# A two-layer hybrid backbone: attention probabilities normalised behind the values' matmuls, and a band mask of the scores' type

## The chip, the cores and the metric

The kernel runs on one core of one Trainium2 chip. The metric is the device time of one execution in microseconds (us). Engines: TensorE (PE, with its weight loads as PEld), VectorE (DVE), ScalarE (ACT), GpSimd (POOL) and SyncE (SP, which issues most DMAs). Each engine works through its own instructions in the order in which the program issues them.

## The reference, cut to what matters

Two consecutive layers on 256 noisy latent tokens with a context of 256 tokens, model width 1024. Each layer is half a SwiGLU, token mixing, and another half SwiGLU, each with RMS norm and a modulation. The even layer mixes with a state-space scan (S5) on half of the width and dense grouped attention on the other half (8 heads of 64, 2 key heads); its context tokens read context alone, its latent tokens read both. The odd layer mixes with windowed grouped attention (16 heads, 4 key heads, a window of 128) with a sink logit per head; only its latent tokens are computed.

```python
def sink_softmax(s, sink):
    sk = jnp.broadcast_to(sink.astype(jnp.float32)[:, :, None, None], s.shape[:-1] + (1,))
    p = jax.nn.softmax(jnp.concatenate([s, sk], axis=-1), axis=-1)
    return p[..., :-1]
...
        s_loc = jnp.where(mi, gqa_scores(qi, ki), -jnp.inf)
        s_ctx = gqa_scores(qi, kc)
        p = sink_softmax(jnp.concatenate([s_loc, s_ctx], axis=-1), sink)
        return gqa_values(p[..., :span], vi) + gqa_values(p[..., span:], vc)
```

The dense attention is the same without mask and sink. All is float32.

## The kernel before

Nearly every large product is made of three float32r matmuls (`mm3`, L392 to L394): each operand is kept as a high part `hi` and the rest `lo`, and hi x hi, hi x lo and lo x hi are summed. Weights come by DMA into a ring of three raw buffers; ScalarE casts the high part (L282), VectorE (in a few cases GpSimd) subtracts for the low part (L300). The order of the work is written out by hand: instructions are issued in program order, and generators on a list `bg` are advanced by one piece at each `tick()`, which is how the scan and the norms are woven between the matmuls.

Both attentions go through `attention`. A unit is 128 queries, two query heads, and two key heads (`kvl`), so it is two sub-units; each has two score tiles. The even layer has eight units (four query tiles; the first two read 256 keys, the others 512), the odd layer eight with 512 keys. A step `s_` of the loop issues, in this order:

- `scores` of sub-unit s: per head two float32r score matmuls (L935, L938) into a PSUM bank of tag `mm` (four bufs), between them in the odd layer a bfloat16 matmul that adds the band mask to one 128-column block (L937), then the row maximum on VectorE (L939);
- `transposes` of sub-unit s - 3: the probabilities by TensorE (L986), the copy `pts` on ScalarE (L987);
- `softmax` of sub-unit s: maxima scaled on VectorE (L951), two exponentials with their sums on ScalarE (L959); then for sub-unit s - 1 the reciprocal of the sums (L971) and the normalisation of its two probability tiles (L974 on ScalarE, L976 on VectorE or GpSimd);
- every second step `values` of a whole unit: 128*64 weights, 256 moving columns into `po`, a bank of tag `ms` (two bufs, shared with the scan's `psS` and `py`), L996; then for each of two heads the high part on VectorE (L1000) and the low part (L1001);
- `tick()`: a piece of the scan in the even layer. Its rotation runs on GpSimd (L1498 to L1504), the scan and its products `pr`, `t` and `H` on VectorE (L1515 to L1529), its matmuls on TensorE (L1470, L1547), copies `Ssb` and `yt` on ScalarE (L1473, L1558). At one of the last ticks (`AH`) ScalarE's casts of the output projection's first weights are issued.

The output projection (`pwo`) follows each attention at once and takes `hi` and `lo` of all units; the last unit gives the third and fourth of the four attention blocks in the even layer, and the last two of eight in the odd layer. The masks are built once, on GpSimd, by `win_masks` (L821 to L832), early in the program, within the scan's preparation.

Of the kernel before, what the change touches and what calls it, by code (L numbers as in the profile page):

```python
# [11 lines left out]
F32 = mybir.dt.float32  # L12
F32R = mybir.dt.float32r
BF16 = mybir.dt.bfloat16
AF = mybir.ActivationFunctionType
OP = mybir.AluOpType
# [10 lines left out]
CTX, LAT = 0, 1  # L27
# [9 lines left out]
def hybrid_kernel(ctx: ExitStack, tc: tile.TileContext, x, c, ctx_in, c_ctx, mod_w, mod_b, norm_g, ffn_wg, ffn_wu,  # L37
# [58 lines left out]
    const = pool("const")  # L96
# [11 lines left out]
    def tt(name, shape, tag=None, bufs=2, dtype=F32):  # L108
        return tmp.tile(list(shape), dtype, name=name, tag=tag or name, bufs=bufs)
# [58 lines left out]
    class Operand:  # L168
# [11 lines left out]

        def __getitem__(self, ix):
            return self.t[ix[2] // 4][ix[:2] + (ix[2] % 4,) + ix[3:]]

    hh, hl = Operand("hh"), Operand("hl")

# [3 lines left out]
    def tokens(t):  # L189

        return t // 2, slice((t % 2) * 128, (t % 2 + 1) * 128)
# [624 lines left out]
                G.tensor_mul(ropeS[:, z, :, hs], rp[:, :, 32:64], gains[:, l, z, None, ho].to_broadcast([128, 2, 32]))  # L816
            G.tensor_scalar(ropeS[:, z, :, 0:32], ropeS[:, z, :, 0:32], -1.0, None, op0=OP.mult)

    masks = const.tile([128, 3, 128], BF16, name="masks")
    sinkb = const.tile([128, 2, 16], F32, name="sinkb")  # L820

    def win_masks():

        mf = tt("mf", [128, 2, 128], tag="half", bufs=3)
        G.memset(mf, 0.0)
        G.affine_select(mf[:, 0], mf[:, 0], pattern=[[-1, 128]], base=0, channel_multiplier=1,
                        compare_op=OP.is_ge, fill=NEG)
        G.affine_select(mf[:, 1], mf[:, 1], pattern=[[1, 128]], base=0, channel_multiplier=-1,
                        compare_op=OP.is_ge, fill=NEG)
        G.tensor_copy(masks[:, 0:2], mf)  # L830
        G.tensor_copy(masks[:, 2], ident)
        G.tensor_scalar(sinkb[:, 1], sinkb[:, 0], -1.0, None, op0=OP.mult)  # L832

    scr = const.tile([128, 1], F32, name="scr")

# [80 lines left out]
    def attention(ap, units, qT, rq, kTh, kTl, v, dst, pt_slots, mask=None, sinkb=None):  # L916


        subs = [(u, kvl) for u in range(len(units)) for kvl in range(2)]
        state = {}  # L920
        pt_n = [0]

        def scores(u, kvl):
            qcol, kvp, hg0, nkb, msk = units[u]
            nk = nkb * 128
            kv = kvp * 2 + kvl
            l = 0 if sinkb is None else 1
            assert ("q", l, (kv * 4 + hg0) // 8 * 8, qcol.start) in ready
            assert all(("k", l, b * 128) in ready for b in range(nkb))
            scs = []  # L930
            mx = tt("mx", [128, 8], bufs=3)
            for i in range(2):
                h = kv * 4 + hg0 + i
                sc = ps("sc")
                T.matmul(sc[:, 0:nk], qT[:, h, qcol], kTh[:, kv, 0:nk], start=True, stop=False)  # L935
                if msk is not None:
                    T.matmul(sc[:, msk[1] * 128:(msk[1] + 1) * 128], mask[:, 2], mask[:, msk[0]], start=False, stop=False)  # L937
                T.matmul(sc[:, 0:nk], qT[:, h, qcol], kTl[:, kv, 0:nk], start=False, stop=True)  # L938
                V.tensor_reduce(mx[:, i:i + 1], sc[:, 0:nk], axis=AX.X, op=OP.max)  # L939
                scs.append(sc)  # L940
            state[u, kvl] = [scs, mx, None]

        def softmax(u, kvl, prev):

            if (u, kvl) in state:
                qcol, kvp, hg0, nkb, msk = units[u]
                nk = nkb * 128
                scs, mx, _ = state[u, kvl]
                hs = slice((kvp * 2 + kvl) * 4 + hg0, (kvp * 2 + kvl) * 4 + hg0 + 2)
                rqu = rq[:, qcol.start // 128]  # L950
                V.tensor_mul(mx[:, 2:4], mx[:, 0:2], rqu[:, 1, hs])  # L951
                if sinkb is not None:
                    V.tensor_tensor(mx[:, 2:4], mx[:, 2:4], sinkb[:, 1, hs], op=OP.min)
                    G.tensor_add(mx[:, 4:6], mx[:, 2:4], sinkb[:, 0, hs])
                sm = tt("smx", [128, 8], bufs=3)
                P = []
                for i in range(2):
                    p = xt_("P", [128, 512])
                    S.activation(p[:, 0:nk], scs[i][:, 0:nk], AF.Exp, bias=mx[:, 2 + i:3 + i],  # L959
                                 scale=rqu[:, 0, hs.start + i:hs.start + i + 1],  # L960
                                 accum_out=sm[:, i:i + 1])
                    P.append(p)
                if sinkb is not None:
                    S.activation(sm[:, 2:4], mx[:, 4:6], AF.Exp)
                state[u, kvl] = [P, sm]
            if prev in state:
                P, sm = state[prev]
                nk = units[prev[0]][3] * 128
                if sinkb is not None:
                    V.tensor_add(sm[:, 0:2], sm[:, 0:2], sm[:, 2:4])  # L970
                V.reciprocal(sm[:, 4:6], sm[:, 0:2])  # L971
                for i in range(2):
                    if sinkb is None and i == 0:
                        S.activation(P[i][:, 0:nk], P[i][:, 0:nk], AF.Copy, scale=sm[:, 4:5])  # L974
                        continue
                    (G if i else V).tensor_scalar(P[i][:, 0:nk], P[i][:, 0:nk], sm[:, 4 + i:5 + i], None, op0=OP.mult)  # L976

        def transposes(u, kvl):
            P, sm = state[u, kvl]
            nkb = units[u][3]  # L980
            pts = pt_slots[pt_n[0] % len(pt_slots)]
            pt_n[0] += 1
            for i in range(2):
                pt = ps("ppt", "tp")
                for kb in range(nkb):
                    T.transpose(pt[:, kb * 128:(kb + 1) * 128], P[i][:, kb * 128:(kb + 1) * 128], ident)  # L986
                S.copy(pts[:, 0:nkb, i * 128:(i + 1) * 128], pt[:, 0:nkb * 128].rearrange("p (b q) -> p b q", b=nkb))  # L987
            state[u, kvl] = pts

        def values(u):  # L990
            qcol, kvp, hg0, nkb, msk = units[u]
            po = ps("po", "ms")
            for kb in range(nkb):
                for kvl in range(2):
                    kv = kvp * 2 + kvl
                    T.matmul(po[kvl * 64:kvl * 64 + 64, 0:256], v[:, kb, kv * 64:kv * 64 + 64], state[u, kvl][:, kb, :],  # L996
                             start=kb == 0, stop=kb == nkb - 1, tile_position=(0, kvl * 64))
            for i in range(2):
                hi, lo = dst(u, i)
                V.tensor_copy(hi, po[:, i * 128:(i + 1) * 128])  # L1000
                V.tensor_sub(lo, po[:, i * 128:(i + 1) * 128], hi.bitcast(F32))  # L1001

        n = len(subs)
        l = 0 if sinkb is None else 1
        TL, dp, sf = TLS[l], DP[l], SF[l]
        for s_ in range(n + TL):
            if s_ < n and sf:
                scores(*subs[s_])
            if s_ >= TL:
                transposes(*subs[s_ - TL])  # L1010
            if s_ < n and not sf:
                scores(*subs[s_])
            c_ = s_ - dp
            if 0 <= c_ <= n:
                softmax(*(subs[c_] if c_ < n else (-1, 0)), subs[c_ - 1] if c_ else None)
            if s_ >= TL + 2 and (s_ - TL) % 2 == 0:
                values(subs[s_ - TL - 2][0])
            tick()
        values(subs[n - 1][0])


# [12 lines left out]
    def s5_prep(pp):  # L1034
# [44 lines left out]
        for _ in range(6):  # L1079
            yield  # L1080
        rope_tables(0)
        win_masks()
        ee = pt_("ee", [128, 1])
        G.memset(ee, math.e)
        dP = pt_("dP", [32, 2])
# [338 lines left out]
    def mixer_ab(nm, ap, nxt):  # L1424
# [220 lines left out]
        for t in range(4):  # L1645
            s_, tl = tokens(t)
            pq = ps("pq")
            for i in range(2):
# [6 lines left out]
                if i:  # L1655
# [3 lines left out]

        units = [(slice(qt * 128, (qt + 1) * 128), 0, hg0, 4 if qt >= 2 else 2, None) for qt in range(4) for hg0 in (0, 2)]  # L1660
        attention(ap, units, qT, rq, kTh, kTl, v,
                  lambda u, i: tuple(z[:, u // 4, 4 + units[u][2] + i, tokens(u // 2)[1]] for z in (hh, hl)),
                  [z[:, s_] for z in (hh.renew(0, F32), hl.renew(0, F32)) for s_ in (CTX, LAT)])
        gc = ap.tile([128, 2, 2, 4, 256], F32R, name="gc", tag="big")

# [93 lines left out]
    def mixer_win(nm, ap, nxt):  # L1759
# [2 lines left out]
        v = ap.tile([128, 4, 256], F32, name="v1")  # L1762
        qT = ap.tile([128, 16, 256], F32R, name="qT1")
        rq = ap.tile([128, 2, 2, 16], F32, name="rq1")
        ckv = [use(("wkv", 0), pre=MW == 0 or WA == 0)]
        pk = [ps("pkv1") for _ in range(4)]
        for s_ in (CTX, LAT):
# [34 lines left out]
                        tick()  # L1802
        if WX:
            warm(AF.Exp)
        units = [(slice(qt * 128, (qt + 1) * 128), kvp, hg0, 4, (0, 3) if qt == 0 else (1, 2))
                 for kvp in range(2) for qt in range(2) for hg0 in (0, 2)]
        attention(ap, units, qT, rq, kTh, kTl, v,
                  lambda u, i: tuple(z[:, LAT, units[u][1] * 4 + units[u][2] + i, units[u][0]] for z in (hh, hl)),
                  [ap.tile([128, 4, 256], F32, name="pts%d" % i) for i in range(4)], mask=masks, sinkb=sinkb)
        fsl = [slice(0, 128), slice(128, 256)]  # L1810
        for dp in range(4):
# [169 lines left out]
```

## Time and profile before

| what | us |
|---|---|
| median of 3 runs (lowest to highest) | 1765.82 (1763.88 to 1766.41) |
| the profiled execution, its time | 1764.65 |
| its span, first to last instruction | 1762.9 |
| TensorE busy in the span | 1710.4 (97%) |
| VectorE busy | 1080.0 (61%) |
| ScalarE busy | 633.9 (36%) |
| GpSimd busy | 425.1 (24%) |

Times in the rows are from the start of the span. The even layer's attention lies from about 519 to 607 us, the odd layer's from about 1480 to 1539. A recorded duration runs to the end of the instruction's last write, so that the next instruction of an engine often starts before it; a step from start to start is what an engine pays. The matmuls' ends are modelled.

### The profile page before, as it was taken

What the parts mean: (1) busy time and instruction counts of PE and PEld (TensorE: products, weight loads), DVE (VectorE), ACT (ScalarE), POOL (GpSimd) and SP (SyncE); (2) the same over time, 40 slices, a digit from 0 to 9 for tenths busy, and PEclk for the clock granted to TensorE, in tenths of its full rate; (3) what the DMA queues carried; (4) which work ended last, traced back from release to release, by engine and by line L of the source; (5) the groups of instructions that cost most, each with busy time, mean ns of one, the idle gap of its engine ahead of it and who ended that gap; (6) DMA issues with size and microseconds to landing.
All of it is one profiled execution on the core that took longest, in us unless ns stands there. A gap on an engine that the chain in (4) does not pass through costs nothing.

```text
span 1762.9 us, 25224 instructions
## 1 busy us (share of the span) xinstructions
PE 1710.4 (97%) x9951; PEld 1430.8 (81%) x9951; DVE 1080.0 (61%) x1802; ACT 633.9 (36%) x1210; POOL 425.1 (24%) x565
## 2 busy tenths in 40 slices
PE   6999999999988899999999999999999998999998
PEld 4778888878976689888888898888888886699998
DVE  5566768566578755576556554754546378755455
ACT  3322222223445643222222243222222257754443
POOL 5314768522367303000000022000000046620000
PEclk8999999999997999999999999999999999999999
DMA  8546575596544524464445323454645224045653
GB/s 261 183 139 173 160 211 178 177 296 215 162 144 131 138 75 166 150 201 136 158 137 162 108 95 114 156 184 145 213 149 163 95 96 96 1 144 169 205 176 120
DMA packets 209454, 272.60 MB, mean 155 GB/s; under 512 B 23673, under 2 KB 171385, under 8 KB 208825
## 3 DMA queue, kind: packets, MB, share of 16 engines
q1 hardware_dynamic: 204912, 261.26, 46.9%
q10 hardware_dynamic: 3064, 5.32, 0.8%
q0 software_dynamic: 1360, 4.42, 0.7%
q8 instruction: 78, 1.28, 0.3%
q14 instruction: 40, 0.32, 0.1%
HBM read 255.77 MB, written 15.17 MB: 154 GB/s over the span
## 4 chain that ended last, share of the span: by engine, by line
PE 84%; DVE 7%; DMA 3%; issue 2%; ACT 2%; POOL 1%; SPq 0%; ACTq 0%; POOLq 0%; DVEq 0%
PE pu L392 16%; PE pu L393 15%; PE pu L394 15%; PE pd L392 7%; PE pd L394 7%; PE pd L393 7%; PE pwo L392 1%; PE pwo L394 1%; PE pwo L393 1%; PE pm L453 1%; PE pacc L392 1%; PE pacc L393 1%; PE pacc L394 1%; DVE H L1529 1%; PE po L996 1%
## 5 line engine op out<-in xcount | busy, mean ns | idle before, releaser
L392 PE MATMUL pu<-hh,whi 128*128 128x512 f32 (+1 forms) x1392 | 505.6, 363 | 3.2 <-ACT hh L549 2.9
L393 PE MATMUL pu<-hl,whi 128*128 128x512 f32 (+1 forms) x1392 | 500.9, 360 | 2.7 <-DVE hl L551 2.6
L394 PE MATMUL pu<-hh,wlo 128*128 128x512 f32 (+1 forms) x1392 | 500.3, 359 | 0.0
L300 DVE TENSOR_TENSOR wlo<-raw,whi 128x1024 fp32r<-128x1024 f32 (+2 forms) x314 | 356.4, 1175 | 42.5 <-ACT whi L282 41.9
L282 ACT CAST whi<-raw 128x1024 fp32r<-128x1024 f32 (+1 forms) x310 | 293.9, 997 | 245.6 <-PE pd L393 158.0
L392 PEld LDWEIGHTS pu<-hh,whi 128*128 128x128 f32 x1392 | 263.7, 189 | 51.2 <-issue 5.3
L393 PEld LDWEIGHTS pu<-hl,whi 128*128 128x128 f32 x1392 | 263.9, 190 | 41.0 <-DVE hl L551 3.5
L394 PEld LDWEIGHTS pu<-hh,wlo 128*128 128x128 f32 x1392 | 263.6, 189 | 39.6 <-DVE wlo L300 0.2
L506 POOL TENSOR_TENSOR acc<-acc,sq 128x256 f32<-128x256 f32 x54 | 41.9, 779 | 784.7 <-ACT sq L512 784.2
L392 PE MATMUL pd<-ahi,whi 128*128 128x512 f32 (+1 forms) x624 | 224.8, 360 | 0.0
L598 DVE TENSOR_TENSOR hm<-sg,pu 128x512 f32<-128x512 f32 (+1 forms) x88 | 54.4, 618 | 275.7 <-PE pu L394 275.6
L394 PE MATMUL pd<-ahi,wlo 128*128 128x512 f32 (+1 forms) x624 | 222.7, 357 | 0.0
L393 PE MATMUL pd<-alo,whi 128*128 128x512 f32 (+1 forms) x624 | 222.6, 357 | 0.0
L227 ACT CAST ahi<-hm 128x512 fp32r<-128x512 f32 (+1 forms) x88 | 49.9, 567 | 367.0 <-DVE hm L598 367.0
L485 DVE SCALAR_TENSOR_TENSOR ma<-mraw,silc,ma 128x1024 f32<-128x1024 f32 (+1 forms) x126 | 142.3, 1160 | 5.7 <-DMA mraw<-in_mod_w_dram 5.4
L392 PEld LDWEIGHTS pd<-ahi,whi 128*128 128x128 f32 x624 | 117.9, 189 | 20.6 <-issue 3.3
L589 DVE SCALAR_TENSOR_TENSOR xT<-pd,m,xT 128x256 f32<-128x256 f32 x192 | 84.6, 478 | 78.6 <-PE pd L394 78.3
L394 PEld LDWEIGHTS pd<-ahi,wlo 128*128 128x128 f32 x624 | 117.9, 189 | 17.6 <-DVE wlo L300 0.5
L393 PEld LDWEIGHTS pd<-alo,whi 128*128 128x128 f32 x624 | 117.9, 189 | 16.5
L594 ACT ACTIVATE sg<-pu 128x512 f32<-128x512 f32 (+1 forms) x88 | 47.6, 544 | 230.0 <-PE pu L394 229.5
L228 DVE TENSOR_TENSOR alo<-hm,ahi 128x512 fp32r<-128x512 f32 (+1 forms) x88 | 56.4, 641 | 55.7 <-ACT ahi L227 55.7
L549 ACT ACTIVATE hh<-h,m 128x256 fp32r<-128x256 f32 x88 | 41.6, 503 | 59.8 <-DVE h L542 59.8
(375 smaller groups left out, 2452.4 us busy)
## 6 DMA issues: line engine op xcount, KB each, us to landing
raw<-in_ffn_wg_dram SPq DMA_DIRECT2D x44, 1024.0 KB, 5.4
raw<-in_ffn_wu_dram SPq DMA_DIRECT2D x44, 1024.0 KB, 5.4
mraw<-in_mod_w_dram SPq DMA_DIRECT2D x72, 512.0 KB, 5.2
raw<-in_mod_w_dram SPq DMA_DIRECT2D x32, 1024.0 KB, 5.1
raw<-in_ffn_wd_dram SPq DMA_DIRECT2D x36, 768.0 KB, 4.5
raw<-in_ffn_wd_dram SPq DMA_DIRECT2D x17, 1024.0 KB, 5.0
raw<-me_d SPq DMA_DIRECT2D x8, 768.0 KB, 5.2
raw<-in_win_w_in_dram SPq DMA_DIRECT2D x6, 1024.0 KB, 5.2
```

The source lines that it names most:

```text
L227: (S.copy if eng is None else eng.tensor_copy)(dst_hi, src)
L228: V.tensor_sub(dst_lo, src, dst_hi.bitcast(F32))
L282: S.copy(ph, src)
L300: eng.tensor_sub(pl_, src, ph.bitcast(F32))
L392: T.matmul(o, lhs[0], rhs[0], start=start, stop=False)
L393: T.matmul(o, lhs[0], rhs[1], start=False, stop=False)
L394: T.matmul(o, lhs[1], rhs[0], start=False, stop=stop)
L485: V.scalar_tensor_tensor(ma[c0, s_], raw[i], silc[:, k, s_:s_ + 1], ma[c0, s_], op0=OP.mult, op1=OP.add)
L506: G.tensor_add(acc[s_], acc[s_], sq_late.pop(s_))
L589: V.scalar_tensor_tensor(xT[:, d, sl], psrc, m[:, l, j, d, s_:s_ + 1], xT[:, d, sl], op0=OP.mult, op1=OP.add)
L594: S.activation(sg, pg, AF.Silu)
L598: V.tensor_mul(hm, sg, pu)
```

## The change

The probabilities stay unnormalised through transposes and values' matmuls. Each unit keeps its inverse sums in a tile `inv` (one per unit, [128, key head, head]). Behind the values' matmuls four small matmuls spread them: the weights are one column of inverse sums repeated 64 times, the moving operand the identity, so that the upper half of `po`'s bank holds, for each of the 64 rows of a head and each query, its inverse sum. The upper half is copied to SBUF (`rb`), multiplied with the lower half into `o`, from which `hi` is copied and `lo` subtracted, each for both heads of the unit in one instruction. In the even layer `rb` and `hi` are copied by ScalarE, in the odd layer by VectorE; the multiplication is VectorE's, the subtraction GpSimd's.

The mask becomes float32r, as the scores are: four blocks (band, zero, band, identity), of which two adjoining ones are added to columns 256 to 511 in one matmul of 256 columns. It is built at the odd layer's start in that layer's pool, on GpSimd; the negated sink alone is still made early.

```diff
+        def pair(self, s_, k, tok):
+            return self.t[k // 4][:, s_, k % 4:k % 4 + 2, tok]
...
+    def win_masks(ap):
+        mf = ap.tile([128, 2, 128], F32, name="mf", tag="pts3")
         G.memset(mf, 0.0)
...
-        G.tensor_copy(masks[:, 0:2], mf)
-        G.tensor_copy(masks[:, 2], ident)
-        G.tensor_scalar(sinkb[:, 1], sinkb[:, 0], -1.0, None, op0=OP.mult)
+        masks = ap.tile([128, 4, 128], F32R, name="masks")
+        for i in range(2):
+            G.tensor_copy(masks[:, 2 - 2 * i], mf[:, i])
+        G.tensor_scalar(masks[:, 1], ident, 0.0, None, op0=OP.mult)
+        G.tensor_copy(masks[:, 3], ident)
+        return masks
...
-                    T.matmul(sc[:, msk[1] * 128:(msk[1] + 1) * 128], mask[:, 2], mask[:, msk[0]], start=False, stop=False)
+                    T.matmul(sc[:, 256:512], mask[:, 3], mask[:, msk:msk + 2], start=False, stop=False)
...
-                V.reciprocal(sm[:, 4:6], sm[:, 0:2])
-                for i in range(2):
-                    if sinkb is None and i == 0:
-                        S.activation(P[i][:, 0:nk], P[i][:, 0:nk], AF.Copy, scale=sm[:, 4:5])
-                        continue
-                    (G if i else V).tensor_scalar(P[i][:, 0:nk], P[i][:, 0:nk], sm[:, 4 + i:5 + i], None, op0=OP.mult)
+                if prev[1] == 0:
+                    inv[prev[0]] = tt("inv", [128, 2, 2], bufs=4)
+                V.reciprocal(inv[prev[0]][:, prev[1]], sm[:, 0:2])
...
+            r = inv.pop(u)
             for i in range(2):
-                hi, lo = dst(u, i)
-                V.tensor_copy(hi, po[:, i * 128:(i + 1) * 128])
-                V.tensor_sub(lo, po[:, i * 128:(i + 1) * 128], hi.bitcast(F32))
+                for kvl in range(2):
+                    T.matmul(po[kvl * 64:kvl * 64 + 64, 256 + i * 128:384 + i * 128], r[:, kvl, i:i + 1].to_broadcast([128, 64]),
+                             ident, start=True, stop=True, tile_position=(0, kvl * 64))
+            rb = tt("rb", [128, 256], tag="acc%d" % (u % 2), bufs=1)
+            (S.copy if sinkb is None else V.tensor_copy)(rb, po[:, 256:512])
+            o = tt("ao", [128, 256], tag="h", bufs=2)
+            V.tensor_mul(o, po[:, 0:256], rb)
+            o = o.rearrange("p (i q) -> p i q", i=2)
+            hi, lo = dst(u)
+            (S.copy if sinkb is None else V.tensor_copy)(hi, o)
+            G.tensor_sub(lo, o, hi.bitcast(F32))
...
         rope_tables(0)
-        win_masks()
+        G.tensor_scalar(sinkb[:, 1], sinkb[:, 0], -1.0, None, op0=OP.mult)
...
         rq = ap.tile([128, 2, 2, 16], F32, name="rq1")
+        masks = win_masks(ap)
         ckv = [use(("wkv", 0), pre=MW == 0 or WA == 0)]
```

## Rows read from the trace of the kernel before

**Rows 1.** Windows: busy time (and count) of each engine, granted clock, DMA.
```profile
570.00:592.00 22.00, 19.37 (x145) 13.45 (x143) 21.42 (x56) 13.59 (x30) 12.66 (x12) 0.92 0.46 120
592.00:608.00 16.00, 13.02 (x110) 9.74 (x109) 8.29 (x23) 13.99 (x28) 4.70 (x3) 0.89 0.46 108
...
1498.00:1530.00 32.00, 32.00 (x232) 21.77 (x230) 28.82 (x96) 28.18 (x76) 20.32 (x22) 1.00 0.01 2
```
**Rows 2.** Chain that ended last, even layer: start, us, what.
```profile
590.10 1.21 DVE mx L939 x2
...
593.24 0.61 ACT P L974
...
602.11 1.31 PE py L1547 x24
...
607.54 0.23 PE pwo L393
```
**Rows 3.** Timeline, one step of the even layer: start, us, engine, line.
```profile
575.22 0.16 DVE L951 TENSOR_TENSOR mx<-mx,rq 128x2 f32<-128x2 f32 x1
...
575.38 0.27 DVE L1000 CAST hh<-po 128x128 fp32r<-128x128 f32 x1
...
576.42 1.26 DVE L1515 TENSOR_TENSOR_SCAN uu<-rhoT,uu 128x256 f32<-128x256 f32 x2
576.91 0.23 ACT L959 ACTIVATION_READ_ACCUMULATOR P<-sc,mx,rq 128x1 f32 x1
...
577.60 0.89 DVE L1524 TENSOR_TENSOR pr<-uu,tbl 128x256 f32<-128x256 f32 x1
```
**Rows 4.** Groups by line, VectorE, 526 to 592: busy, mean ns, idle before.
```profile
L1525 DVE TENSOR_TENSOR t<-uu,tbl 128x256 f32<-128x256 f32 x12 | 7.3, 610 | 0.0
L1524 DVE TENSOR_TENSOR pr<-uu,tbl 128x256 f32<-128x256 f32 x12 | 6.9, 573 | 0.0
...
L1000 DVE CAST hh<-po 128x128 fp32r<-128x128 f32 x10 | 2.8, 278 | 2.7 <-PE po L996 2.7
```
**Rows 5.** Groups by line, ScalarE, 515 to 608.
```profile
L1558 ACT COPY yt<-py 128x256 f32<-128x256 f32 x8 | 2.6, 380 | 0.0
```
**Rows 6.** Timeline, a VectorE operation with one operand in PSUM.
```profile
1424.52 0.47 DVE L542 SCALAR_TENSOR_TENSOR h<-xT,m,pn 128x256 f32<-128x256 f32 x1
```
**Rows 7.** Timeline, GpSimd's normalisation beside a VectorE product.
```profile
572.05 1.83 POOL L976 TENSOR_SCALAR P<-P,smx 128x512 f32<-128x512 f32 x1 [2.49 <-PE po L996]
572.11 0.42 DVE L1525 TENSOR_TENSOR t<-uu,tbl 128x256 f32<-128x256 f32 x1
```
**Rows 8.** Line 554, a GpSimd subtraction: ns min/median/max.
```profile
L554 POOL TENSOR_TENSOR hl<-h,hh x18: 728/742/1605, 445.0 to 1571.8; 128x256 fp32r<-128x256 f32 x18
```
**Rows 9.** Timeline, the even layer's tail.
```profile
600.80 2.00 ACT L282 CAST whi<-raw 128x1024 fp32r<-128x1024 f32 x2
...
604.05 1.07 ACT L987 COPY hl<-ppt 128x512 f32<-128x512 f32 x2 [1.25 <-PE ppt L986]
...
607.04 0.50 PE L392 MATMUL pwo<-hh,whi 128*128 128x512 f32 x1
```
**Rows 10.** Timeline, one masked score and the transposes behind it.
```profile
1502.34 0.40 PE L935 MATMUL sc<-kTh,qT 128*128 128x512 f32 x1
...
1502.94 1.03 PE L986 MATMUL ppt<-ident,P 128*128 128x128 f32 x8
```
**Rows 11.** Chain, the odd layer's output projection (256 columns).
```profile
1538.99 0.32 PE pwo L392
...
1541.22 0.12 PE pwo L394
```
**Rows 12.** Timeline of GpSimd, three places; brackets: idle time before, releaser.
```profile
41.79 0.76 POOL L1087 TENSOR_TENSOR dP<-ee,lsP 32x2 f32<-32x2 f32 x1 [7.51 <-DMA lsP<-in_s_log_step_dram]
...
1433.58 0.70 POOL L553 TENSOR_TENSOR h<-h,m 128x256 f32<-128x256 f32 x1 [2.46 <-ACT hh L549]
...
1538.02 4.75 POOL L300 TENSOR_TENSOR wlo<-raw,whi 128x1024 fp32r<-128x1024 f32 x2 [3.97 <-ACT whi L282]
```

More of the change, by code (lines that the diff above doesn't have):

```diff
@@ L817, in rope_tables @@
             G.tensor_scalar(ropeS[:, z, :, 0:32], ropeS[:, z, :, 0:32], -1.0, None, op0=OP.mult)
-    masks = const.tile([128, 3, 128], BF16, name="masks")
     sinkb = const.tile([128, 2, 16], F32, name="sinkb")
-    def win_masks():
-        mf = tt("mf", [128, 2, 128], tag="half", bufs=3)
+    def win_masks(ap):
+        mf = ap.tile([128, 2, 128], F32, name="mf", tag="pts3")
         G.memset(mf, 0.0)
@@ L919, in attention @@
         subs = [(u, kvl) for u in range(len(units)) for kvl in range(2)]
-        state = {}
+        state, inv = {}, {}
         pt_n = [0]
@@ L967, in softmax @@
                 P, sm = state[prev]
-                nk = units[prev[0]][3] * 128
                 if sinkb is not None:
                     V.tensor_add(sm[:, 0:2], sm[:, 0:2], sm[:, 2:4])
-                V.reciprocal(sm[:, 4:6], sm[:, 0:2])
-                for i in range(2):
-                    if sinkb is None and i == 0:
-                        S.activation(P[i][:, 0:nk], P[i][:, 0:nk], AF.Copy, scale=sm[:, 4:5])
-                        continue
-                    (G if i else V).tensor_scalar(P[i][:, 0:nk], P[i][:, 0:nk], sm[:, 4 + i:5 + i], None, op0=OP.mult)
+                if prev[1] == 0:
+                    inv[prev[0]] = tt("inv", [128, 2, 2], bufs=4)
+                V.reciprocal(inv[prev[0]][:, prev[1]], sm[:, 0:2])
         def transposes(u, kvl):
@@ L1661, in mixer_ab @@
         attention(ap, units, qT, rq, kTh, kTl, v,
-                  lambda u, i: tuple(z[:, u // 4, 4 + units[u][2] + i, tokens(u // 2)[1]] for z in (hh, hl)),
+                  lambda u: tuple(z.pair(u // 4, 4 + units[u][2], tokens(u // 2)[1]) for z in (hh, hl)),
                   [z[:, s_] for z in (hh.renew(0, F32), hl.renew(0, F32)) for s_ in (CTX, LAT)])
@@ L1804, in mixer_win @@
             warm(AF.Exp)
-        units = [(slice(qt * 128, (qt + 1) * 128), kvp, hg0, 4, (0, 3) if qt == 0 else (1, 2))
+        units = [(slice(qt * 128, (qt + 1) * 128), kvp, hg0, 4, 1 - qt)
                  for kvp in range(2) for qt in range(2) for hg0 in (0, 2)]
         attention(ap, units, qT, rq, kTh, kTl, v,
-                  lambda u, i: tuple(z[:, LAT, units[u][1] * 4 + units[u][2] + i, units[u][0]] for z in (hh, hl)),
+                  lambda u: tuple(z.pair(LAT, units[u][1] * 4 + units[u][2], units[u][0]) for z in (hh, hl)),
                   [ap.tile([128, 4, 256], F32, name="pts%d" % i) for i in range(4)], mask=masks, sinkb=sinkb)
```

## The prediction

> **What bounds the kernel now.** I read the windows first, since the change touches two short stages and an average over the span says nothing of them. In the grid attention of the odd layer TensorE is the bound: from 1498 to 1530 it is busy for the whole of the stretch [rows 1], so there each matmul added costs its length and each normalisation removed on another engine gives nothing. In the dense attention of the even layer it is another engine: VectorE is busy for 21.42 of 22 us from 570 to 592, TensorE for less, and only from 592 on does VectorE fall to 8.29 of 16 [rows 1]. The chain of waits agrees: it runs on VectorE up to the row maxima at 590.10, then goes over to ScalarE (the normalisation at 593.24 is on it) and to TensorE, which it stays on from 602 to the output projection [rows 2]. VectorE is full there because the state-space scan of the other head group runs in the same steps.
>
> So three things have to be priced: VectorE's time in the even layer, the tail of that layer, and TensorE's time in the odd layer.
>
> **The even layer, VectorE's order.** Before, a pair of heads leaves VectorE four instructions: they start at 575.38, just behind the row maximum's scaling at 575.22, and the next scan starts at 576.42 [rows 3], so a unit takes 1.04 us. They read only the values' bank, which was long done. Now one multiplication stands in this place. It needs `rb`, and ScalarE copies `rb` in program order behind the two exponentials of the same step, which themselves wait for VectorE's scaling at 575.22. In the trace those exponentials' last sum is read at 576.91 and ends at 577.14 [rows 3]; I take the next free place at 577.0, since recorded ends overlap the next start. A ScalarE copy of 128x256 out of PSUM takes 0.38 [rows 5], a VectorE operation of 128x256 with one operand in PSUM 0.47 [rows 6]. The multiplication would end near 577.85, and VectorE's queue goes on 1.4 us later than before: the wait costs more than the three saved instructions. What is queued behind it is the scan, its products and the next row maxima, on which ScalarE's exponentials wait in turn.
>
> Five units have their copies before 592 (ten casts) [rows 4]. In one of them VectorE waited 2.7 us for TensorE anyway [rows 4]: I count nothing there. Two have 512 keys: 2 x 1.4. Two have 256 keys, where the exponentials are shorter: I take 1.0 each (estimate). Sum +4.8 us. From below, if the copy were always ready first, each unit would save 1.04 - 0.47 = 0.57, five units -2.9.
>
> **GpSimd's relief.** The products `pr` and `t` take 0.573 and 0.610 us in the mean [rows 4], against 0.42 for one that meets nothing of the kind [rows 7]; the one at 577.60, which meets a product on GpSimd, took 0.89 [rows 3]. Over 12 of each that is 1.8 and 2.3, together about 4.1 us that VectorE loses beside GpSimd. The change takes 16 multiplications off GpSimd here, and the rotation's products run earlier, part of them inside VectorE's new waits. But a subtraction of 0.74 us [rows 8] per unit comes to GpSimd, with two operands in SBUF as the rotation's products have. The bounds are 0 and 4.1; I take -2.5, nearer to the upper, since the waits are empty time.
>
> What the removed multiplication itself did to VectorE is seen at 572.05: it ran 1.83 us, and the VectorE product that started 0.06 us later took 0.42 [rows 7], no more than undisturbed. The Trainium skill, "SBUF — State Buffer", section "SBUF: two separate sides", says that VectorE operations with two SBUF inputs and GpSimd operations exclude one another, the later one waiting for the whole of the earlier. By that rule the product would have waited until 573.88; this row disagrees for this pair, while the row at 577.60 agrees for two products. If the rule held for all, the removal would free more of VectorE than I count (the second rival).
>
> **The even layer's tail.** ScalarE's normalisation of 0.61 on the chain at 593.24 goes [rows 2]: -0.6. Then ScalarE's order matters. Two casts of the output projection's weights ran at 600.80 for 2.00 us, while TensorE was still at the last but one unit, and the last transposes' copy came at 604.05 [rows 9]. These casts are issued in the same step behind `values`. Now `rb` and `hi` of that unit stand before them, and `rb` waits for the values and the broadcasts. The scan's output matmuls follow these values on TensorE from 602.11 [rows 2], so with 0.22 for the broadcasts they end near 602.3; `rb` 0.38, the multiplication 0.47, `hi` 0.38 and three handovers bring the casts to 603.7 to 605.7, and the last copy starts there and not at 604.05: +1.65. The last four broadcasts lie on TensorE's path: +0.25. The projection began at 607.04 on a step of 0.23 [rows 9, 2]; its seventh weight pair needs the last unit's `lo`, which now comes behind copy, multiplication, copy and 0.74 us on GpSimd, 2.3 us with handovers, where TensorE arrives after 1.4 to 1.6: +0.6. Tail: -0.6 + 1.65 + 0.25 + 0.6 = +1.9.
>
> Even layer: 4.8 - 2.5 + 1.9 = +4.2 us.
>
> **The odd layer.** Four broadcasts per unit, 128*64 weights with 128 moving columns in float32: the scan's output matmuls have that form, 24 in 1.31 us [rows 2], 0.055 each. Eight units: 32 x 0.055 = +1.8. From above, the transposes of 128x128, eight in 1.03 [rows 10], 0.13 each: +4.1. Below this there is nothing to hide it, TensorE has no idle time. A rule would put it higher: the Trainium skill, "FP8 and Floating Point Precision", section "TensorE Precision Notes", gives true float32 four passes; by that 128 columns would take 4 x 128 / 2.4 GHz = 0.21 us and a unit, with two halves side by side, 0.43, and the sum would be 1.6 higher. The 0.055 of this kernel's own rows disagrees.
>
> The mask: a score with its mask takes 0.60 us from start to start (1502.34 to 1502.94) [rows 10], two score matmuls at 0.23 [rows 2] leave 0.14 for the bfloat16 mask and what it does to its neighbours' weight loads. The new one has 256 float32r columns; that form runs at 0.12 in the projection [rows 11]. 32 masks: -0.6. From above, if it takes a full 0.23, +2.9. The removed normalisations on VectorE and GpSimd and the copies that become a multiplication lie under TensorE: 0. At the end of this stage the new chain is some 2 us long and TensorE has 18 matmuls of 0.12, 2.2 us, before it wants the last pair: 0, with no cover left. The weights' second parts on GpSimd (4.75 us for two from 1538.02) [rows 12] now queue behind `lo` and end about 3 us later, near 1546. The projection starts at 1539.0 and, 48 matmuls of 0.12 and then 15 more later [rows 11], wants their second half near 1546.5: 0, and up to 2 if it is later.
>
> Odd layer: 1.8 - 0.6 = +1.2 us.
>
> **Building the masks.** Early, GpSimd waited 7.51 us for a DMA at 41.79 behind this code [rows 12]: moving it away gives 0. In the odd layer GpSimd idled 2.46 us before 1433.58 [rows 12], and seven operations (a memset, two selects, four copies) of some 0.3 each fit there: 0, and at most 0.5 if they start late, when the norm's operations queue behind them.
>
> **Sum.** 4.2 + 1.2 = +5.4 us on the profiled execution's 1764.65, that is 1770.0. The profiled execution lies 1.2 below the median of 1765.82, inside the spread of the runs; the difference is 0.3%. A change of 0.2%, 3.5 us, is about what a measurement here tells from none.
>
> **Rivals.** One: faster. VectorE lags behind ScalarE at every unit, so that `rb` is ready when the multiplication's turn comes. Then five units give -2.9 in place of +4.8 and GpSimd's relief comes whole, 4.1: -2.9 - 4.1 + 1.9 + 1.2 = -3.9, 1760.8. For it speaks that ScalarE loses 16 normalisations here; against it that the exponentials start from VectorE's own result of the same step, so ScalarE can't be ahead. It decides once VectorE comes to the multiplication some 2 us (575.4 to 577.4) later in the step than now. Chance 0.15.
>
> Two: no difference. The wait is there, but the relief is whole, and as large again on the scan's writes of `H` (an estimate, as they meet the same products): 8.2 in place of 2.5, 5.4 - 5.7 = -0.3, 1764.4. This is what the page's lock would come to here, bounded by what VectorE's rows have in excess. With partial relief (from 4.4) it ends below 0.2% too. Chance 0.28.
>
> Three: slower still. In the odd layer the broadcasts and the mask cost their upper bounds: +2.3 and +3.5 more, 1775.8. For it speaks that TensorE has no slack there; against it, that both forms have rows of their own. Chance 0.10.
>
> My forecast, 1770.0, has 0.47. Its own range is 1768.2 to 1773. The range for all but 2 in 10 reaches into the second rival and part of the third: 1763 to 1775. Slower by over 0.2%: 0.57, within 0.28, faster 0.15.
>
> **What would show it.** VectorE should stand idle some 1 to 1.5 us before each multiplication in the even layer, with ScalarE's `rb` as releaser; the weights' casts should start behind the last but one `hi`, TensorE should wait about 0.6 at the projection's start; `pr` and `t` should be shorter in the mean. In the odd layer each unit's cycle should grow by about 0.15, with the mask's step near 0.12. I am wrong if VectorE waits for nothing there, or if the odd layer's stage changes by more than 3 us.

## The result, and the profile after

The changed kernel takes 1788.03 us (median of four runs, 1786.23 to 1788.69) against 1765.11 before (one run more than ahead of the prediction): ratio 1.0127, 95% interval [1.0115, 1.0139]. The forecast was 1770.0: slower as it said, but by 23 us and not by 5, and outside its range. The profiled execution took 1788.33 (span 1786.5, 23.6 more than before).

Where the span grew is found by laying the two traces' matmuls side by side: how much later does the same matmul start in the changed kernel? The lag, in us:

| Matmul (start before) | lag | grown in this stretch |
|---|---|---|
| keys and values of the even layer (520) | 3.1 | 3.1, in the down-projections of the first feed-forward layer, 1.4 of it in one jump at 229 |
| last scan matmuls beside the even layer's attention (598) | 7.8 | 4.7 |
| first of the even layer's output projection (607.04, [rows 9]) | 11.3 | 3.5 |
| end of that projection (649) | 12.4 | 1.1 |
| end of the two middle feed-forward layers (1425) | 17.8 | 5.4, in their down-projections |
| the odd layer's norm (1436) | 19.5 | 1.7 |
| first of the odd layer's output projection (1538.99, [rows 11]) | 22.3 | 2.8 |
| end | 23.6 | 1.3, in the last feed-forward layer |

So 9.8 of the 23.6 us (3.1 + 5.4 + 1.3) lie in layers in which the change doesn't touch an instruction. The jump at 229 is TensorE waiting for the split of the hidden activations on ScalarE and VectorE; the other 8.4 us creep up matmul by matmul. The even layer lost 9.3, the odd layer 4.5.

The windows answer to [rows 1]: busy time of TensorE, weight loads, VectorE, ScalarE, GpSimd, then the granted clock, over the same work.

```profile
576.50:601.00 24.50, 19.21 (x151) 12.78 (x151) 20.27 (x45) 12.20 (x29) 10.23 (x13) 0.94 0.41 107
601.00:619.30 18.30, 13.78 (x140) 10.22 (x139) 7.04 (x19) 12.03 (x27) 1.45 (x2) 0.99 0.52 126
1517.80:1551.80 34.00, 34.00 (x272) 26.98 (x270) 23.99 (x77) 28.51 (x76) 5.62 (x16) 1.00 0.01 1
```

VectorE, full in this stage before, now idles 4.2 of 24.5 us; TensorE is still full in the odd layer, and takes 34 us for what took 32. What VectorE waits for stands in its groups by line (529 to 603), which answer to [rows 4]:

```profile
L1540 DVE TENSOR_TENSOR H<-pr,t 64x128 f32<-64x128 f32 (+2 forms) x39 | 18.9, 511 | 0.7
...
L1535 DVE TENSOR_TENSOR pr<-uu,tbl 128x256 f32<-128x256 f32 x12 | 7.2, 596 | 0.0
L1536 DVE TENSOR_TENSOR t<-uu,tbl 128x256 f32<-128x256 f32 x12 | 7.1, 592 | 0.0
...
L1008 DVE TENSOR_TENSOR ao<-po,rb 128x256 f32<-128x256 f32 x5 | 2.1, 424 | 10.6 <-ACT rb L1006 10.6
```

10.6 us of idle time before five multiplications, all ended by ScalarE's `rb`; `pr` and `t` are not shorter. In the kernel before, the ten subtractions that stood beside the ten casts of [rows 4] were:

```profile
L1001 DVE TENSOR_TENSOR hl<-po,hh 128x128 fp32r<-128x128 f32 x10 | 2.9, 292 | 0.3
```

One unit in the timeline (it answers to [rows 3, 7]; the step has two exponentials):

```profile
569.65 0.82 ACT L965 ACTIVATE P<-sc,mx,rq 128x512 f32<-128x512 f32 x1
569.81 1.07 PE L1003 MATMUL po<-ident,inv 128*64 128x128 f32 x8
...
570.93 0.37 ACT L1006 COPY rb<-po 128x256 f32<-128x256 f32 x1 [0.36 <-PE po L1003]
...
571.40 0.42 DVE L1008 TENSOR_TENSOR ao<-po,rb 128x256 f32<-128x256 f32 x1 [3.74 <-ACT rb L1006]
...
571.86 0.40 ACT L1011 CAST hh<-ao 128x256 fp32r<-128x256 f32 x1 [0.56 <-DVE ao L1008]
...
572.34 1.18 POOL L1012 TENSOR_TENSOR hl<-ao,hh 128x256 fp32r<-128x256 f32 x1 [4.79 <-ACT hh L1011]
...
573.48 0.91 POOL L1509 TENSOR_TENSOR uu<-Ssb,tbl 128x256 f32<-128x256 f32 x1
```

Read it downwards: exponentials, `rb`, multiplication, cast, subtraction are one chain over ScalarE, VectorE, ScalarE and GpSimd. At its end GpSimd has stood 4.79 us with the subtraction at the head of its queue, and the scan's rotation (L1509), which has nothing to do with it, starts behind it. The eight broadcasts took 1.0 us here, as TensorE's granted clock was 0.50, its lower level, from 568 to 572 after it had waited 3.6.

The chain that ended last now passes over ScalarE's `rb` in seven of the eight units, where before it ran along VectorE [rows 2]:

```profile
580.50 1.30 DVE mx L945 x2
582.02 1.63 ACT P L965 x4
583.65 0.27 ACT rb L1006
583.98 0.30 issue
584.28 1.26 DVE uu L1526 x2
...
606.26 0.27 ACT rb L1006
606.55 0.44 DVE ao L1008
607.01 0.40 ACT hh L1011
607.42 0.49 ACT hh L989
607.96 1.14 PE ppt L988 x8
609.10 1.88 PE po L998 x16
610.98 0.44 PE po L1003 x8
```

From 606.26 on it is the tail: even the copy of the transposes (L989) now stands behind `rb`, multiplication and cast. The tail in the timeline (answers to [rows 9]):

```profile
612.73 0.41 ACT L1011 CAST hh<-ao 128x256 fp32r<-128x256 f32 x1 [0.56 <-DVE ao L1008]
613.04 1.99 ACT L286 CAST whi<-raw 128x1024 fp32r<-128x1024 f32 x2
...
614.93 1.06 ACT L989 COPY hl<-ppt 128x512 f32<-128x512 f32 x2
...
618.35 0.50 PE L396 MATMUL pwo<-hh,whi 128*128 128x512 f32 x1
...
620.72 0.50 PE L397 MATMUL pwo<-hl,whi 128*128 128x512 f32 x1 [0.30 <-POOL hl L1012]
```

One unit of the odd layer on TensorE (answers to [rows 10]), first before, then after. From `po` at 1523.71 to the next score at 1526.02 it is 2.31 us; the same stretch took 1.88 before (1510.10 to 1511.98). A score with its mask takes 0.58 (1526.71 to 1527.29), 0.60 before [rows 10].

```profile
1510.10 1.95 PE L996 MATMUL po<-pts,v 128*64 128x256 f32 x16
1511.98 0.50 PE L935 MATMUL sc<-kTh,qT 128*128 128x512 f32 x1
```

```profile
1523.71 1.95 PE L998 MATMUL po<-pts,v 128*64 128x256 f32 x16
1525.49 0.61 PE L1003 MATMUL po<-ident,inv 128*64 128x128 f32 x8
1526.02 0.50 PE L941 MATMUL sc<-kTh,qT 128*128 128x512 f32 x1
...
1526.71 0.40 PE L941 MATMUL sc<-kTh,qT 128*128 128x512 f32 x1
1526.94 0.28 PE L943 MATMUL sc<-masks 128*128 128x256 f32 x1
1527.06 0.39 PE L944 MATMUL sc<-kTl,qT 128*128 128x512 f32 x1
1527.29 1.03 PE L988 MATMUL ppt<-ident,P 128*128 128x128 f32 x8
```

GpSimd at the start of the odd layer (answers to [rows 12]): the mask build fits into no gap. It follows L558, and the norm's power L535, for whose result TensorE waits, follows it:

```profile
1452.20 0.84 POOL L558 TENSOR_TENSOR hl<-h,hh 128x256 fp32r<-128x256 f32 x1
1452.97 0.31 POOL L828 MEMSET mf<- 128x256 f32 x1
...
1454.85 0.28 POOL L837 CAST masks<-ident 128x128 fp32r<-128x128 f32 x1
1455.10 0.72 POOL L535 TENSOR_TENSOR rr<-rs,mhalf 128x2 f32<-128x2 f32 x1
```

Last, a line that no change was made to: 88 matmuls of the last feed-forward layer (shortest, median and longest duration in ns, then the first and the last start), of the kernel before and then of the changed one. From the first to the last of them, 163.0 us became 164.2.

```profile
L392 PE MATMUL pacc<-whi,ahi x88: 389/389/396, 1594.1 to 1757.1; 128*128 128x512 f32 x88
```

```profile
L396 PE MATMUL pacc<-whi,ahi x88: 390/393/404, 1616.7 to 1780.9; 128*128 128x512 f32 x88
```

### The profile page after: what moved, and what is told of

Its sections match the earlier page's. It is cut to its first block, busy times and chain, and to the rows that moved or that the text cites. A ratio compares the mean times of both kernels' runs of the same rounds, so it can differ in the third digit from the quotient of the medians.

```text
span 1786.5 us, 25343 instructions
## 1 busy us (share of the span) xinstructions
PE 1725.5 (97%) x10079; PEld 1441.2 (81%) x10079; DVE 1071.8 (60%) x1754; ACT 631.7 (35%) x1210; POOL 385.6 (22%) x551
## 4 chain that ended last, share of the span: by engine, by line
PE 84%; DVE 8%; ACT 3%; DMA 2%; issue 2%; POOL 1%; SPq 0%; POOLq 0%; ACTq 0%; DVEq 0%
PE pu L396 15%; PE pu L397 15%; PE pu L398 15%; PE pd L396 7%; PE pd L398 7%; PE pd L397 7%; PE pwo L397 1%; PE pwo L396 1%; PE pwo L398 1%; DVE H L1540 1%; PE pm L457 1%; PE pacc L398 1%; PE pacc L397 1%; PE pacc L396 1%; DMA me_d<-Et 1%
## 5 line engine op out<-in xcount | busy, mean ns | idle before, releaser
L553 ACT ACTIVATE hh<-h,m 128x256 fp32r<-128x256 f32 x88 | 41.6, 503 | 61.1 <-DVE h L546 61.1
```

## The experiments

### The layers that were not changed: placement in SBUF

SBUF is the memory in which the tiles lie. The masks left the constants (768 bytes of a partition) and the inverse sums came to the small tiles (128). Every tile allocated behind them moved: the weights' `whi` by 768 bytes, the feed-forward layers' hidden activations `ahi` by 640. By the sizes of the tiles in the program their distance was a multiple of 512 and is now 128 more than one.

**The change with the addresses of before:**

```diff
+    G.memset(const.tile([128, 160], F32, name="padc"), 0.0)
...
-                    inv[prev[0]] = tt("inv", [128, 2, 2], bufs=4)
+                    inv[prev[0]] = const.tile([128, 2, 2], F32, name="inv", bufs=4)
```

> The changed kernel with 640 bytes of filler in the constants and the inverse sums' four buffers beside them: every tile from the residual stream to the hidden activations then lies at the address it had before the change; the instructions are the same. Placement theory (the 9.8 us that the feed-forward layers lost come from where the operands lie in SBUF): the down-projections' 512-column matmuls return from 229 to 226 ns and the time to about 1778 us (1788.0 - 9.8). Rival (the feed-forward layers lose time to something else that the change brought, and the addresses are a coincidence): the time stays at 1788 and the 229 ns stay.

1778.81 us, ratio to before 1.0078 [1.0063, 1.0093]: 9.2 less. In the feed-forward layers the lag no longer creeps up (7.9 us at 649 and at 1425; the others show single jumps of 0.4 and less), and the line above is back at 163.1 us:

```profile
L396 PE MATMUL pacc<-whi,ahi x88: 389/389/396, 1608.5 to 1771.6; 128*128 128x512 f32 x88
```

Placement holds, the rival falls. Its odd layer lost 4.5 us where the changed kernel lost 2.8: around its first scores TensorE's clock was granted at 0.79 and 0.87 (five-us windows), where the kernel before had 1.00. The excess lies there: from 1480 to 1500 the lag grows by 2.0, in the changed kernel by 0.4.

```profile
1495.00:1500.00 5.00, 2.14 (x9) 0.79 0.06 13
1500.00:1505.00 5.00, 4.90 (x25) 0.87 0.00 0
```

**The kernel before, moved.** The same fillers, in its constants (`padc`) and behind its small tiles (`padt`), and nothing else. 256 bytes in the constants and 128 behind the small tiles:

```diff
+    G.memset(tmp.tile([128, 32], F32, name="padt"), 0.0)
+    G.memset(const.tile([128, 64], F32, name="padc"), 0.0)
```

> The kernel before, with 256 bytes of filler in the constants and 128 behind the small tiles: no instruction of the change, but modulo 1024 the operands lie as in the changed kernel. Placement theory: the down-projections slow to 229 ns and the time rises from 1765 to about 1775 (3.1 + 5.4 + 1.3 us, and perhaps 1 more in attention). Rival (not placement, or placement in units other than 1024 bytes): 1765.

1773.5, ratio 1.0045 [1.003, 1.006]. Only the 128 bytes behind the small tiles, so that the hidden activations move and the weights stay:

> The kernel before, with 128 bytes of filler behind the small tiles only: the hidden activations move by 128 bytes and the weights stay. If the down-projections' moving operand is what counts (by its own address or by its distance to the weights), about 1775 as in the run above; if the weights' address counts, 1765.

1771.82, ratio 1.0038 [1.0023, 1.0053], like the run above below the 1775 expected. 128 bytes in the constants, so that all of them move together:

> The kernel before, with 128 bytes of filler in the constants: weights, hidden activations and residual stream all move by 128 bytes and keep their distances. If the distance between the two operands counts, 1765; if the address of the moving operand itself counts, about 1775, and the gate and up projections (whose operands move too this time) may slow as well.

1764.11, ratio 0.9996 [0.9986, 1.0006]: nothing. So it is not the address of the hidden activations that counts but their distance to tiles ahead of the filler; the weights, which the slowed matmuls read with them, are among these. Then three more distances, by 64, 256 and 512 bytes behind the small tiles:

> The kernel before, with 64 bytes of filler behind the small tiles: the distance from the weights to the hidden activations becomes 64 modulo 512 (0 in the kernel before, 128 in the changed one). If any distance that is no multiple of 512 (or of 256) slows the down-projections: 1770 to 1774, 229 ns. If only some do: 1765.

> The same with 256 bytes: distance 256 modulo 512. If the unit is 256 bytes (or less), 1765 and 226 ns; if it is 512, 1770 to 1774.

> The same with 512 bytes: distance 0 modulo 512 and 512 more modulo 1024. If the unit is 512 bytes or less, 1765; if it is 1024, 1770 to 1774.

With 64 bytes 1768.78, ratio 1.0021 [1.0011, 1.003], below the 1770 to 1774 expected of a loss; with 256 bytes 1764.9, 1.0002 [0.9993, 1.0012]; with 512 bytes 1764.62, 1.0001 [0.9992, 1.001]. The line of the 88 matmuls with 64 and then with 256 bytes:

```profile
L392 PE MATMUL pacc<-whi,ahi x88: 393/398/398, 1597.0 to 1761.4; 128*128 128x512 f32 x88
```

```profile
L392 PE MATMUL pacc<-whi,ahi x88: 389/389/396, 1595.5 to 1758.6; 128*128 128x512 f32 x88
```

164.4 and 163.1: of the distances tried, multiples of 256 bytes cost nothing, 64 and 128 cost 4 and 7 us. The step from one start to the next tells the same: over 1275 steps of the 512-column down-projections of the first three feed-forward layers the median is 227 ns in the kernel before and with 256, 512 and all moved, 232 in the changed kernel and in the two runs with 128, and 229 with 64. In the last layer it goes from 227 to 232 with 128 and to 235 with 64. (The 229 ns of the expectations is the most frequent step with 128, not the middle one; many are at 237 and 238.) Why the hardware does so no run shows.

### The parts of the change, with the addresses of before

All that follow start from the run at 1778.8. **The mask build issued later**, behind the keys' and values' projections:

```diff
-        masks = win_masks(ap)
         ckv = [use(("wkv", 0), pre=MW == 0 or WA == 0)]
...
+        masks = win_masks(ap)
         for hf in range(2):
             pq = [ps("pq1") for _ in range(2)]
```

> The changed kernel with the addresses of before, and the building of the band masks issued behind the keys' and values' projections instead of ahead of them. Theory (the build's 2.1 us on GpSimd stand ahead of the norm's power L535, for which TensorE waits at the start of the odd layer): L535 starts again within some 0.5 us of its input, the 1.7 us at the start of that layer go, time 1778.8 - 1.7 = 1777.1. Rival (GpSimd is loaded there too, and the build only delays the keys' norms): 1778.8.

1777.53, ratio 1.0074 [1.0059, 1.0089]. The two intervals overlap, so the times alone settle nothing; the trace does: L535 starts 0.43 us behind L558, and the lag over this stretch goes from 9.69 to 9.66 where it had grown by 1.7.

```profile
1444.03 0.83 POOL L558 TENSOR_TENSOR hl<-h,hh 128x256 fp32r<-128x256 f32 x1
1445.30 0.71 POOL L535 TENSOR_TENSOR rr<-rs,mhalf 128x2 f32<-128x2 f32 x1 [0.43 <-DVE rs L533]
```

**One layer normalised as before, the other as changed** (the condition for the first run; the second has `is not None`; the end of `values` branches alike):

```diff
+                if sinkb is None:
+                    nk = units[prev[0]][3] * 128
+                    V.reciprocal(sm[:, 4:6], sm[:, 0:2])
...
+                else:
+                    if prev[1] == 0:
...
```

> The changed kernel with the addresses of before, and the even layer normalised as before the change (probabilities scaled on ACT and GpSimd, the two copies and subtractions on DVE out of the bank): the odd layer's part and the masks alone. If the layers' losses stand side by side, the even layer gives back its 8.1 us: 1770.7. Rival (a good part of these 8.1 us does not come from the even layer's new normalisation): above 1774.

> The changed kernel with the addresses of before, and the odd layer normalised as before the change, the new masks left in: the even layer's part and the masks alone. By eight units at 0.40 us the odd layer gives back 3 us, and up to 4.5 with the slow start of its first units in the run that is compared: 1774.3 to 1775.8. Rival (the 0.40 us of a unit come from the wider masks, not from the broadcasts): 1778.8.

The odd layer's part alone: 1770.91, ratio 1.0036 [1.0023, 1.0049], 7.9 us less than both. The even layer's part alone: 1775.92, ratio 1.0065 [1.005, 1.008], 2.9 less. The losses add. In the second run the lag grows by 1.1 at the first scores of the odd layer and then stays within 0.2 over seven units: the wider mask costs nothing there, and the 0.40 us a unit are the broadcasts'.

**Broadcasts by transposes**, four instructions in place of eight:

```diff
-                for kvl in range(2):
-                    T.matmul(po[kvl * 64:kvl * 64 + 64, 256 + i * 128:384 + i * 128], r[:, kvl, i:i + 1].to_broadcast([128, 64]),
-                             ident, start=True, stop=True, tile_position=(0, kvl * 64))
+                for kvl, pr in ((1, 128), (0, 64)):
+                    T.transpose(po[0:pr, 256 + i * 128:384 + i * 128], r[:, kvl, i:i + 1].to_broadcast([128, pr]), ident)
```

> The changed kernel with the addresses of before, and the inverse sums spread by transposes (one over 128 rows, one over the lower 64, for each half) instead of four float32 matmuls, each of which is two instructions of TensorE: four instructions for a unit instead of eight. Theory (the broadcasts cost what their instructions cost, 0.53 us a unit): 0.27 us a unit, 2.1 us less in the odd layer, and less than 1 in the even layer, which is bound by waits: 1776 to 1777. Rival (the broadcasts hide behind DVE's waits, and the unit's 0.40 us come from elsewhere): 1778.8.

1780.14, ratio 1.0093 [1.0073, 1.0112]: no gain, against the 1776 to 1777 expected. The unit in its timeline:

```profile
1522.32 1.95 PE L999 MATMUL po<-pts,v 128*64 128x256 f32 x16
1524.20 0.65 PE L1004 MATMUL po<-ident,inv 128*128 128x128 f32 x4
1524.60 0.47 PE L942 MATMUL sc<-kTh,qT 128*128 128x512 f32 x1
```

2.28 us from `po` to the next score, against 2.31: a transpose costs 0.10 where an instruction of the float32 matmul on half the columns costs 0.05. Halving the count halves nothing.

### The even layer: which wait

Base: the run with the late mask build, 1777.5. **GpSimd's subtraction one step later:**

```diff
-            G.tensor_sub(lo, o, hi.bitcast(F32))
+            held.append(lambda: G.tensor_sub(lo, o, hi.bitcast(F32)))
...
         for s_ in range(n + TL):
+            while held:
+                held.pop(0)()
```

> The changed kernel with the addresses of before and the masks built late (1777.5 us measured), and in the even layer GpSimd's subtraction of the low part issued at the start of the next step, but for the last unit. Theory A (the loss sits on GpSimd: at the head of its queue the subtraction waits for the cast on ACT, 3.7 us before 567.99, with the scan's rotation products queued behind it, and these then run late beside VectorE): the products start some 3 us earlier at that unit, and 4 to 6 us of the even layer's 8 to 9 go: 1772 to 1773.5. Theory B (the loss is VectorE's own wait for the copy rb on ACT, 12.5 us by the rows of the changed kernel): at most 1 us goes, 1776.5 to 1777.5.

**`rb` copied by VectorE, the subtraction where it was:**

```diff
-            (S.copy if sinkb is None else V.tensor_copy)(rb, po[:, 256:512])
+            V.tensor_copy(rb, po[:, 256:512])
```

> The same base, and in the even layer the broadcast sums are copied by VectorE itself, as in the odd layer, instead of by ACT; the cast of the high part stays on ACT. Theory B (VectorE's wait for ACT): VectorE waits for TensorE alone again and pays 0.42 us a unit for the copy: 3 to 5 us go, 1772.5 to 1774.5. Theory A (GpSimd's queue behind the cast, which still stands behind the exponentials on ACT): at most 1 us goes, 1776.5 to 1777.5.

**Copy, multiplication, cast and subtraction one step later** (the same list, holding all four):

> The same base, and in the even layer everything behind the broadcasts (copy, multiplication, cast, subtraction) issued at the start of the next step, but for the last unit. Both waits go: by A and B alike the even layer keeps only its broadcasts and its tail, some 1 to 3 us, and the time is 1770 to 1772. If neither wait is what costs (rival C: TensorE's lower clock and the broadcasts themselves), 1776 or more.

They gave 1774.82 (ratio 1.006 [1.0045, 1.0075]), 1770.28 (1.0031 [1.002, 1.0042]) and 1768.44 (1.0023 [1.0013, 1.0033]): 2.7, 7.2 and 9.1 us back. The first lies between its two theories, the others 2.2 and 1.6 us below the ranges expected. The first's interval overlaps the base's [1.0059, 1.0089].

The times also hold something that is not the even layer's. In all three traces the stretch of lower clock between the two middle feed-forward layers, near 1062, is shorter than in the base, and the lag falls by 1.6 there (granted clock from 1064 to 1084, by ten us: 0.81 and 0.85 in the base, 0.83 and 1.00 in the first of the three). So the traces are read for the even layer alone, as the growth of the lag from 520 to 649: 9.4 in the base (8.1 to 9.4 in the runs whose even layer is the changed kernel's), then 6.6, 1.0 and 2.2.

VectorE's waits from 526 to 606, in the base and in the second of them (total, times, longest):

```profile
DVE ao L1009 <- ACT rb L1007: 12.1, 6, 3.3
```

```profile
DVE rb L1007 <- PE po L1004: 7.0, 2, 5.2
```

Six waits for ScalarE became two for TensorE, and the kernel before has two there as well (7.7 us, one of them in [rows 4], the other in the tail). Theory B is right: the copy's place behind the exponentials is what costs, more than I expected of it. The gain lies ahead of the tail: by the last scan matmuls (598) the lag has grown by 5.4 in the base and has shrunk by 2.9 with the copy on VectorE, while the tail from there to 649 costs 4.0 and 3.9. Only the run with all four later shortens the tail, to 1.7, though VectorE still waits 8.6 us for `rb` in it, three times.

GpSimd's queue is real but second: moving the subtraction gives 1.5 to 2.8 us by the lag while B's wait stands, and VectorE's scan, `pr`, `t` and `H` take 52.5 us from 500 to 620 in place of the base's 54.6. With that wait gone the move gives nothing that shows, as the last run says.

**The best of the parts.** The even layer as in the third of these runs, the odd layer's normalisation as before, the mask late:

> The even layer as in the run above, the odd layer's normalisation as before the change, the masks new and built late, the addresses of before: the best that the parts found so far make. If the parts add, 2.9 us (the odd layer's part as measured) below the run above: 1767 to 1769, no better than the kernel before, since the even layer gains nothing by the change. Rival (GpSimd and ACT, freed of the normalisations, give time back once the waits are gone): under 1764.

1765.65, ratio 1.0004 [0.9995, 1.0014]: no difference from the kernel before, and less than the 1767 to 1769 expected, by about the 1.6 us near 1062 that its trace shows too. **The same with `rb` on VectorE and only the subtraction later:**

> The even layer with the copy of the broadcast sums on VectorE and GpSimd's subtraction issued in the next step, the odd layer's normalisation as before the change, the new masks built late, the addresses of before: both waits of the even layer removed at their cheapest. From the run with the copy on VectorE (1770.3), 2.9 us less for the odd layer and up to 2 less for the subtraction: 1765.4 to 1767.4. Rival (once the waits are gone, the relief of GpSimd and ACT that the prediction had counted at 2.5 us shows): 1761 to 1763, faster than both kernels.

1767.25, ratio 1.0017 [1.0007, 1.0026], what the parts add up to (1770.3 - 2.9). With the waits removed or shortened at two prices, neither kernel beats the one before. From 520 to 598 the lag shrinks by 1.8 and 0.6 (by 0.6 also in the kernel before with 512 bytes of filler), and the tail costs 1.8 and 3.1 again. GpSimd's relief is not in it: VectorE's scan, `pr`, `t` and `H`, 53.6 us before, take 54.9 and 55.5.

## Why the prediction was wrong

The direction was right, and so were several sizes; that the kernel became slower is no proof of the sum, since the largest part of the loss stands in none of its terms. Point by point, with the forecast of each term:

- **VectorE's wait: right.** Forecast: `rb` some 2.0 us behind the place of the old copies in units of 512 keys, 1.4 net; 1.0 net with 256. Measured in the changed kernel: 1.89 to 1.94 and 1.51 to 1.52 of idle time. The unit counted at nothing, because it waited 2.7 already, waited 3.74. All five: 10.6 - 2.7 of idle time more, and 5.7 - 2.1 of instructions less, +4.3 us against a forecast of +4.8. The run with the copy on VectorE shows that this wait is what costs.
- **GpSimd's relief: the first step that failed.** Forecast -2.5; `pr` and `t` together went from 14.2 to 14.3 us, and `H` grew from 466 to 511 ns in the mean of the same 39. The sentence that the products would "run earlier, part of them inside VectorE's new waits" had it the wrong way round: the subtraction waits at the head of GpSimd's queue for the end of the same chain, the rotation runs later, and when VectorE goes on it meets it. What was queued behind the added instruction was asked for VectorE and ScalarE in the even layer, not for GpSimd. The products of the runs with the waits removed or shortened are no shorter either; only the subtraction moved by itself brings scan, `pr`, `t` and `H` below the kernel before, by 1.1 us.
- **The even layer's tail: +4.6 for +1.9.** The casts' 1.65 was right (1.57). The normalisation that left ScalarE did not give -0.6: `rb`, the multiplication and the cast took its place ahead of the transposes' copy, +1.0. The broadcasts of two units lie on the path at 0.5 and 0.44, not one at 0.25. The stalls in the projection came to 1.1 for 0.6. (The chain before does not stay on TensorE from 602, as the prediction reads it: ScalarE's copy at 604.05 [rows 9] is on it.)
- **The odd layer: +2.8 for +1.2.** The broadcasts were mis-sized: 0.43 us a unit (2.31 - 1.88) for 0.22. The row used was right, 0.055 for an instruction of that form; the count was not. A float32 matmul of the program is two instructions in the trace (x8 for a unit's four), as the values' x16 for eight matmuls show. The Trainium skill, "FP8 and Floating Point Precision", "TensorE Precision Notes", gives true float32 four passes, from which the prediction estimated 0.43 a unit; it set the trace against that, and the trace, rightly counted, agrees with it. The mask is a little cheaper than the old one (0.58 for 0.60 a score), as forecast, and its range's upper end was not touched.
- **The mask build: +1.7 for 0.** The gap of 2.46 us that was to take it lies ahead of L553 (L557 in the changed kernel); the code issues the build behind the subtraction L558 that follows, next to the power on which the norm hangs. The idle time was real, but not at this place in the queue. The late build shows it.
- **Untouched layers: +9.8, in no term and no rival.** The largest part: the prediction put them at nothing without a reason. It priced instructions alone; that tiles allocated anew move all others was not asked. Of the 9.8, 8.4 creep up in the down-projections as placement makes them, and the runs with moved tiles give 7 to 9 for it. The jump of 1.4 at 229 is not shown to be placement.

The rivals: VectorE never came to the multiplication after `rb`, so the first fell; the relief of the second, 8.2, came in no run; the third was half right, in that the broadcasts went towards their upper bound (3.5 for 4.1). Of the two signs of being wrong neither came by its letter: VectorE did wait, and the odd layer's stage grew by 2.8, under 3 (4.5 with the mask build). By the lags, the even layer up to its tail, the tail, the odd layer, the mask build and the untouched layers make 4.7 + 4.6 + 2.8 + 1.7 + 9.8 = 23.6 us, the growth of the span.

## What to carry to other kernels

A change that adds, drops or moves a tile shifts every tile allocated behind it: compare the same untouched matmuls in both traces before explaining a difference by the change, and try a filler that restores the addresses. For an instruction added to a chain over several engines, write down for each of them what stands behind it in program order: here a copy cheap in itself cost 7 us by its place behind two exponentials, and a mask build cost 1.7 by its place ahead of a power. And count a matmul's instructions in the trace, not in the program.

## What the runs showed of the hardware

The 512-column float32r matmuls of the down-projections run slower when the hidden activations lie 64 or 128 bytes further from the weights in SBUF than in the kernel before, where the distance is a multiple of 512: with 128 their median step from one start to the next went from 227 to 232 ns, that is 7 to 9 us of this kernel; at 0, 256 and 512 bytes, and when both move together by 128, nothing is lost. The down-projections of 256 columns kept their step of 120 ns. So did the gate and up projections, whose operands kept their distance, with 226. That it is the distance to the weights, and not to another tile ahead of the filler, is argued: the slowed matmuls read these two, and no run moves the weights alone.
